# Where the operands of the matmuls lie in on-chip memory: start addresses by role, modulo 512 bytes

## The chip, the cores and the metric

The kernel runs on one core of a Trainium2 chip. The metric is the device time of one execution in microseconds (us); lower is better. The time before is 1484.54 us, the median of 3 runs.

## The reference: what is computed

Two encoder layers over 512 tokens of width 1024. Each layer adds a normed token mixer and a normed SwiGLU channel mixer; layer 0 mixes by neighbourhood attention, layer 1 by dilated attention in three groups.

```python
def reference(x, ...):
    for layer in range(DEPTH):
        j = layer // N_MIXERS
        h = rms_norm(x, norm_mix_pre[layer])
        if layer % N_MIXERS == 0:
            h = neighbourhood_attention(h, na_w_qkv[j], na_w_o[j], na_rpb[j])
        else:
            h = dilated_attention(h, dil_w_qkv[j], dil_w_o[j])
        x = x + rms_norm(h, norm_mix_post[layer])
        h = rms_norm(x, norm_ffn_pre[layer])
        x = x + rms_norm(swiglu(h, ffn_w_gate[layer], ffn_w_up[layer], ffn_w_down[layer]), norm_ffn_post[layer])
    return x
```

All of it is fp32. The sizes that count are the projections: D_MODEL 1024, D_FF 2816 (22 tiles of 128).

## The kernel before

**The products.** Every large product is done in three matmuls. `split` (L364) makes of an fp32 value a high part in the float32r format (ScalarE, L365) and the rest, also float32r (VectorE, L366). `mm3` (L376) then multiplies high by high (L377), high by low (L378) and low by high (L379):

```python
def mm3(o, s, m, start, stop):
    i = pe.matmul(o, s[0], m[0], start=start, stop=False, skip_group_check=True)
    pe.matmul(o, s[0], m[1], start=False, stop=False, skip_group_check=True)
    pe.matmul(o, s[1], m[0], start=False, stop=stop, skip_group_check=True)
```

The first operand, `s`, is the stationary one: its 128 columns are loaded as weights before each matmul (engine row PEld). The second, `m`, is the moving one: 256 or 512 columns stream through. While one matmul streams its moving operand, the weights of the next are read. On top of that, 2x2 blocks of a product are formed with seven products where eight would be usual (class `Seven`, L405, and `Values`, L479); four of the seven are `d1`, `s2`, `s4`, `s3` with operand sums.

**The stages**, in order, for each layer: the mixer (value products, then per head pair the query and key products `pp`, scores, softmax, transposes, values), the out-projection (`out_proj`, tiles `yo`), gate and up (`gate_up`, tiles `gu`, 22 units of 7 products of 12 matmuls of 256 columns: 1,848 matmuls) and down (`down`, tiles `yd_s` and `yd_pp`, 462 matmuls of 512 columns). The out-projection has 192 matmuls of 512 columns.

**The order of the work** on each engine is found by a planner (class `Order`, L131): it simulates the program with costs from `_cost` (L77) several times and pins the best order it found (L1441). It reads which columns of which buffer an instruction touches; it knows nothing of addresses.

**The places.** Buffers lie side by side on each partition in the order in which the pools are opened: first `ident` and `mhalf` (L306 to L308), then `rxa` (transposed activations of the moving side, L323), `rxc` (the same, and other things by stage, L324), `vmem` (L325), `mem` (L327), small values, then `wpool`: two raw weight buffers and eight slots for split weights (`wslot`, L369; tiles named `h_..` and `l_..`). The rest is an arena that grows from the left (`rxb`, `raw`) and from the right (`akl`, `ao`, `wm`, `memc`). The constant `mhalf` (128x1) takes 32 bytes, so that every buffer behind it starts 32 bytes past a multiple of 64. A piece of a buffer that a matmul reads starts at a multiple of 512 bytes from the buffer's start, with few exceptions (the queries of layer 0's odd heads: 256 more). So a matmul operand's start modulo 512, its residue below, is that of its buffer.

**Roles.** In `Seven`, stationary operands are weights (`wslot`, or `vmem` and the end of `rxc` for the product `s4`, by `w22_ring`, L347) and moving ones are activations (`rxa`, `rxc`, `rxb`). In `Values` and `v_quarter` it is the other way round. In `out_proj` the activations `rv` (in `rxa`) are stationary, the weights moving. In `down` the stationary operands are the activations split into `hl_` (L1047, in `rxc`), the moving ones are weights in `wslot`.

Of the kernel before, what the change touches and what calls it, by code (L numbers as in the profile page):

```python
# [13 lines left out]
F32 = mybir.dt.float32  # L14
F32R = mybir.dt.float32r
# [3 lines left out]
P = 128  # L19
SEQ = 512  # L20
D = 1024
# [7 lines left out]
COLS = 64  # L29
ROWS = 8  # L30
EPS = 1e-6
MEM, ARENA = 14544, 9 * D
NEG = -1e30
BIG = 3.0e38
X1A, X1B, X2B, D1, S2, S4, S3 = range(7)
BANKS = {"pp": 3, "s": 2, "t": 2, "o": 1}
SLOPES = [float(np.float32(2.0) ** np.float32(-8.0 * (h + 1) / HEADS)) for h in range(HEADS)]

# [258 lines left out]
def encoder_kernel(ctx: ExitStack, tc: tile.TileContext, a: dict, out: bass.AP):  # L297
    nc = tc.nc
    act, dve, pool, pe = nc.scalar, nc.vector, nc.gpsimd, nc.tensor

    cpool = ctx.enter_context(tc.tile_pool(name="cpool", bufs=1))
    wpool = ctx.enter_context(tc.tile_pool(name="wpool", bufs=4))
    psum = ctx.enter_context(tc.tile_pool(name="psum", bufs=1, space=bass.MemoryType.PSUM))
    dpool = ctx.enter_context(tc.tile_pool(name="dpool", bufs=1, space=bass.MemoryType.DRAM))

    ident = cpool.tile([P, P], F32, name="ident")  # L306
    make_identity(nc, ident)
    mhalf = cpool.tile([P, 1], F32, name="mhalf")  # L308
    dve.memset(mhalf, -0.5)
    spill = [dpool.tile([NT, P, D], F32, name=f"spill{i}") for i in range(3)]  # L310

    tags, arenas, extra = {}, [], []
# [1 line left out]
    def tagged(pool_, shape, dtype, tag, name, bufs):  # L314
        v = pool_.tile(shape, dtype, tag=tag, name=name, bufs=bufs)
        tags.setdefault(tag, ([], bufs))[0].append(v.tensor.name if hasattr(v, "tensor") else v.name)
        return v
# [4 lines left out]

    rxa = cpool.tile([P, 10 * D], F32R, name="rxa")  # L323
    rxc = cpool.tile([P, 5 * D + 256], F32R, name="rxc")  # L324
    vmem = cpool.tile([P, D], F32R, name="vmem")  # L325

    mem = cpool.tile([P, MEM], F32, name="mem")  # L327
    rvd = [dpool.tile([PAIRS, P, D], F32, name=f"rvd{i}") for i in range(2)]

    tops = {"left": 0, "right": 0}  # L330
# [1 line left out]
    @contextmanager  # L332
    def arena(name, n, side="left", dtype=F32):
        with tc.tile_pool(name=f"p_{name}", bufs=1, side=side) as pool_:
            v = pool_.tile([P, n], dtype, name=name)
            at = tops[side]
            tops[side] += n
            mine = [v.tensor.name if hasattr(v, "tensor") else v.name, at, at + n, len(arenas), None, side]
            arenas.append(mine)
            yield v  # L340
            mine[4] = len(arenas)
            tops[side] -= n

    def ring(mem, start, n, bufs):
        return cycle([mem[:, start + i * n:start + (i + 1) * n] for i in range(bufs)])

    def w22_ring(mem):  # L347
        return cycle([hl(vmem, 0, 512), hl(mem, 0, 512)])

    small_ = cycle(range(20))  # L350

    def small(name, n=1):
        if "o0" in name or "o1" in name:
            return tagged(cpool, [P, n], F32, f"small_o{next(small_)}", name, 1)
        return tagged(cpool, [P, n], F32, f"small{n}", name, 16 if n > 1 else 12)

    def load2(srcs, name, raw=None):
# [461 lines left out]
    def gate_up(layer, xs, hid, more, rings, sums):  # L819
        wg, wu = a["wg"], a["wu"]  # L820
        raws = ring(more, 0, 2 * D, 3)
        g_, u_, p5_ = rings
        v_ = w22_ring(rxc[:, 4 * D:5 * D])
        units, us = {}, {}

        def unit_of(f):
            if f in units or f >= FT:
                return units.get(f)
            raw = load2((wg[layer, f], wu[layer, f]), f"gu{layer}_{f}", None if f % 5 < 2 else next(raws))
            b, g = bank(("s", "s", "pp", "o", "pp", "pp")[f % 6], f"gu{layer}_{f}"), next(g_)  # L830

            def sink(n, left, other):
                u = us.get(f)
                if n == 0:
                    act.activation(g[:, :256], other, AF.Copy)
                    dve.tensor_add(g[:, :256], g[:, :256], left)
                elif n == 1:
                    act.activation(u[:, :256], other, AF.Copy)
                    dve.tensor_sub(u[:, :256], u[:, :256], left)  # L839
                elif n == 2:  # L840
                    dve.tensor_sub(u[:, 256:], other, left)
                else:
                    act.activation(g[:, :256], g[:, :256], AF.Silu)
                    act.activation(g[:, 256:], left, AF.Silu)
                    dve.tensor_mul(hid[f], *(v.rearrange("p (h c) -> p h c", h=2) for v in (g, u)))

            units[f] = Seven(raw, b, xs, f"{layer}_{f}", sink, None, next(v_), (pool, pool, dve, dve))
            return units[f]

        ahead, early = 3, 5  # L850
        for f in range(early):
            unit_of(f).first()
        for f in range(FT):
            for i in range(f, min(f + 2, FT)):
                if i not in us:
                    us[i], units[i].p5 = next(u_), next(p5_)
            run(unit_of(f), unit_of(f + 1), unit_of(f + ahead) if f + ahead >= early else None)
            if sums and (f < 16 or f % 2 == 0):
                sums.pop(0)(units[f].added)
# [151 lines left out]
    def hl(mem, i, n):  # L1011
        return mem[:, i * D:i * D + n], mem[:, i * D + n:i * D + 2 * n]
# [6 lines left out]
    xs = {i: op4(rxa, 2 * n) for n, i in enumerate((D1, S2, S4, S3, X2B))} | {X1A: op4(rxc, 0), X1B: op4(rxc, 2)}  # L1019
# [17 lines left out]
    def mix_out(layer, w, rxb, wm, load_x):  # L1037
        for j in range(PAIRS - 1):
            nc.gpsimd.dma_start(rxa[:, j * D:(j + 1) * D], rvd[layer][j])

        us = [None] * 2 + [hl(wm, 0, D), (wm[:, 2 * D:], vmem), hl(rxa, 8, D)] + [hl(rxb, 2 * i, D) for i in range(3)]

        out_proj(w, rv, layer, load_x, us, (ring(mem, 4 * D, D, 4), ring(mem, 0, D, 4), ring(mem, 13440, 512, 2)),
                 (mem[:, 11392:11392 + D], mem[:, 12416:12416 + D]))

    def ffn(layer, stack, memc):
        hl_ = ring(rxc, 0, D, 5)  # L1047
        rxb = None
        hm = mem[:, :FT * 512]
        h2 = hm.rearrange("p (h x) -> p h x", h=2)  # L1050
        hid = [h2[:, :, f * 256:f * 256 + 256] for f in range(FT)]
        with arena(f"raw{layer}", 6 * D) as more:
            gate_up(layer, xs, hid, more, (ring(memc, 0, 512, 5), cycle([memc[:, 2560:3072], mem[:, 13520:14032]]), ring(mem, MEM - 512, 256, 2)),
                    sums[layer])
            rcomb = ring(memc, 2 * D, 512, 2)

            def sink(t, xt, hs, gn):
                if layer == 1:
                    for n in range(2 if t == NT - 1 else 1):
                        s = slice(512 * n, 512 * n + 512) if t == NT - 1 else ALL  # L1060
                        (nc.sync, act)[n].dma_start(out[t][:, s], xt[:, s])
                else:
                    nc.sync.dma_start(spill[1][t], xt)
                    prenorm(hs[t], xt, gn, f"n{layer}_{t}")
                    operands(mixer_operands(rxb) if rxb is not None else None, x, hs, t, rcomb, f"n{layer}_{t}")

            end = down(layer, hm, hl_, memc[:, :2 * D], more, sink)
        if layer == 0:
            rxb = stack.enter_context(arena("rxb1", 6 * D, dtype=F32R))
        end()  # L1070
        return rxb
# [5 lines left out]
    rxb = stack.enter_context(arena("rxb0", 6 * D, dtype=F32R))  # L1077
# [23 lines left out]
    ost_, w22_ = ring(ao, 0, D, 1), w22_ring(ao[:, D:2 * D])  # L1101
# [3 lines left out]
    q_, k_, kl_ = ring(rxc, 0, 1152, 2), ring(rxc, 2304, D, 2), cycle([zero_rows(v) for v in (akl, rxc[:, 4352:])])  # L1105
    vq = [v_quarter(apv[:, qd * D:(qd + 1) * D], a["na_v"][qd], f"n{qd}",
                    raw0 if qd == 0 else None) for qd in range(4)]
    qs, ks, us = {}, {}, {}
# [36 lines left out]
             lambda v: v.rearrange("p (i c) -> p i c", i=ROWS))  # L1145

    inner.close()
    with arena("wm0", 3 * D, "right", F32R) as wm:
        mix_out(0, a["na_o"], rxb, wm, lambda xt, t: nc.sync.dma_start(xt, a["x_rows"][t]))
    stack.close()  # L1150
    memc = inner.enter_context(arena("memc0", 3 * D, "right"))
# [9 lines left out]
    pt_, few_ = ring(ap, 10 * D, D, 4), ring(mem, 0, 96, 2)  # L1161
    bt, qs, ks = memc[:, 0:1536].rearrange("p (k c) -> p k c", c=P), memc[:, 1536:2048], memc[:, 2048:2560]
    p5_ = ring(memc, 2560, 256, 2)
    q_, k_, kl_, ost_ = rxc[:, 0:D], rxc[:, D:2 * D], rxc[:, 2 * D:3 * D], ring(rxc, 3 * D, D, 1)
    w22_ = w22_ring(rxc[:, 4 * D:5 * D])
    def by_token(v):

        return v.rearrange("p (m r) -> p r m", r=4)
# [188 lines left out]
    order = [3 * j + g for j in range(PAIRS) for g in orders[j]]  # L1357
    stats, parts, weight, pts, vg, ready, left, later = {}, {}, {}, {}, {}, [], {}, {}

    vus, vslots = {}, cycle([hl(rxc, 0, D), hl(rxc, 2, D), (vmem, rxc[:, 4 * D:5 * D])])  # L1360
    for qd in range(2):
        v = v_quarter(ap[:, (6 + qd) * D:(7 + qd) * D], a["dil_v"][0, qd], f"d{qd}")
        nc.sync.dma_start(vd[0][qd].rearrange("t p c -> p t c"), v)
# [63 lines left out]
                nc.sync.dma_start(xt[32 * r + 16:32 * r + 32], rows[r, 0:16])  # L1427

    inner.close()
    with arena("wm1", 3 * D, "right", F32R) as wm:  # L1430
        mix_out(1, a["dil_o"], rxb, wm, load_block)
    stack.close()
    memc = inner.enter_context(arena("memc1", 3 * D, "right"))
# [90 lines left out]
```

## Time and profile before

| | before |
|---|---|
| median of 3 runs | 1484.54 us (1484.52 to 1489.98) |
| the profiled execution's own time | 1487.69 us |
| span in the profile | 1485.9 us |
| granted TensorE clock | 0.996 |
| PE busy | 1442.8 us (97%), 10788 instructions |
| DVE busy | 1196.8 us (81%) |
| ACT busy | 904.1 us (61%) |
| POOL busy | 542.4 us (37%) |

PE is TensorE's matmuls, PEld its weight loads, DVE VectorE, ACT ScalarE, POOL GpSimd. Matmuls overlap each other in the records (each has a modelled end), so what a matmul costs is not its duration but the time from its start to the next one's start; this distance is called the pace here. A row of the timeline has the start in us, the duration in us, engine, line, operation, and what is written from what: `gu<-rxa,h_b` writes bank `gu` from buffers `rxa` and `h_b`; two buffers of the same name are shown once. The windows table has for each stretch its length, then for each engine its busy time and in brackets its instructions, those that reach in over an edge counted too.

### The profile page before, as it was taken

The page shows a single profiled execution, that of the slowest core. Times are in us where ns is not written, and L with a number is a line of the kernel's source. Part 1 is how long each engine was busy: PE and PEld are TensorE (multiplying, and loading weights), DVE is VectorE, ACT ScalarE, POOL GpSimd, SP SyncE. Part 2 cuts the span into 40 slices and gives each one's busy share as a digit, 9 for nine tenths or more (in the row PEclk, how much of TensorE's full clock was granted, in tenths as well). Part 3 has the DMA queues.
Part 4 walks back from the last instruction along what each step waited for, and adds up shares of the span by engine and source line. Part 5 has one row for each costly group of instructions (what it writes and reads, how often), then busy time and mean ns, then how long its engine had stood idle before and what let it go on. Part 6 is the DMA issues. An engine that isn't in the chain of part 4 may idle for free.

```text
span 1485.9 us, 27934 instructions
## 1 busy us (share of the span) xinstructions
PE 1442.8 (97%) x10788; PEld 1333.1 (90%) x10788; DVE 1196.8 (81%) x1876; ACT 904.1 (61%) x1819; POOL 542.4 (37%) x398
## 2 busy tenths in 40 slices
PE   7999999899999999999999999999999999999997
PEld 6988877899999888899999999989977999999886
DVE  5499967699889788797689788787657989998877
ACT  4478874555555567544467778876675654555664
POOL 5345425544231001665555444334204644330001
PEclk9999999899999999999999999999999999999999
DMA  5346487677333664435433343333766788834662
GB/s 200 139 177 179 155 286 206 227 221 212 114 112 114 204 220 162 168 126 187 142 100 101 93 145 116 100 133 103 237 206 214 200 243 243 252 126 149 203 208 92
DMA packets 86645, 253.22 MB, mean 170 GB/s; under 512 B 19312, under 2 KB 31600, under 8 KB 84464
## 3 DMA queue, kind: packets, MB, share of 16 engines
q1 hardware_dynamic: 77696, 197.69, 40.4%
q0 software_dynamic: 8672, 53.48, 13.9%
q8 instruction: 85, 1.39, 0.4%
q14 instruction: 48, 0.39, 0.1%
q10 hardware_dynamic: 144, 0.26, 0.0%
HBM read 229.24 MB, written 68.29 MB: 200 GB/s over the span
## 4 chain that ended last, share of the span: by engine, by line
PE 77%; DVE 8%; ACT 7%; DMA 3%; issue 3%; POOL 1%; SPq 0%; POOLq 0%; DVEq 0%; ACTq 0%
PE gu L377 10%; PE gu L378 9%; PE gu L379 9%; PE pp_d L377 5%; PE pp_d L379 4%; PE pp_d L378 4%; PE yd_s L377 3%; PE yd_s L379 3%; PE yd_s L378 3%; PE yd_pp L377 2%; PE yd_pp L379 2%; PE yd_pp L378 2%; PE sb L1274 2%; PE yo L377 2%; PE yo L379 1%
## 5 line engine op out<-in xcount | busy, mean ns | idle before, releaser
L585 POOL TENSOR_TENSOR rs_yd<-v_yd,mhalf 128x1 f32<-128x1 f32 x8 | 8.3, 1043 | 261.3 <-DVE v_yd L583 261.3
L378 PE MATMUL gu<-rxa,h_b 128*128 128x256 f32 x352 | 100.0, 284 | 2.5 <-DVE rxa L602 2.5
L377 PE MATMUL gu<-rxc,h_a 128*128 128x256 f32 x352 | 99.7, 285 | 2.0 <-ACT h_a L365 1.2
L377 PE MATMUL gu<-rxa,h_c 128*128 128x256 f32 x352 | 99.7, 283 | 1.3 <-DVE memc L839 1.1
L378 PE MATMUL gu<-rxc,h_a 128*128 128x256 f32 x352 | 99.7, 284 | 1.2 <-DVE rxc L602 1.0
L377 PE MATMUL gu<-rxa,h_b 128*128 128x256 f32 x352 | 99.7, 284 | 1.2 <-ACT rxa L601 1.2
L379 PE MATMUL gu<-rxa,l_b 128*128 128x256 f32 x352 | 99.6, 283 | 0.2 <-DVE l_b L366 0.2
L379 PE MATMUL gu<-rxc,l_a 128*128 128x256 f32 x352 | 99.1, 282 | 0.0
L378 PE MATMUL gu<-rxa,h_c 128*128 128x256 f32 x352 | 98.7, 280 | 0.0
L379 PE MATMUL gu<-rxa,l_c 128*128 128x256 f32 x352 | 98.3, 280 | 0.0
L365 ACT ACTIVATE rxc<-mem 128x512 fp32r<-128x512 f32 (+2 forms) x90 | 55.9, 624 | 65.9 <-PE yd_pp L378 33.8
L445 POOL TENSOR_TENSOR r_d<-r_d 128x512 f32<-128x512 f32 x24 | 36.1, 1506 | 161.0 <-DVE l_ad L366 122.9
L445 POOL TENSOR_TENSOR r_gu<-r_gu 128x512 f32<-128x512 f32 x20 | 30.6, 1529 | 149.8 <-DVE l_a L366 102.4
L366 DVE TENSOR_TENSOR rxc<-mem,rxc 128x512 fp32r<-128x512 f32 (+2 forms) x90 | 64.4, 719 | 19.5 <-ACT rxc L365 19.2
L445 POOL TENSOR_TENSOR raw<-raw 128x512 f32<-128x512 f32 x24 | 38.0, 1582 | 99.4 <-DVE l_a L366 74.7
L378 PEld LDWEIGHTS gu<-rxa,h_b 128*128 128x128 f32 x352 | 67.6, 192 | 2.7 <-DVE rxa L602 2.7
L377 PEld LDWEIGHTS gu<-rxc,h_a 128*128 128x128 f32 x352 | 67.1, 192 | 2.8 <-ACT h_a L365 1.4
L377 PEld LDWEIGHTS gu<-rxa,h_c 128*128 128x128 f32 x352 | 66.5, 189 | 2.9 <-DVE memc L839 1.3
L378 PEld LDWEIGHTS gu<-rxc,h_a 128*128 128x128 f32 x352 | 67.2, 191 | 1.8 <-DVE rxc L602 1.8
L377 PEld LDWEIGHTS gu<-rxa,h_b 128*128 128x128 f32 x352 | 67.3, 192 | 1.5 <-ACT rxa L601 1.4
L1238 ACT ACTIVATE mem<-mem 128x256 f32<-128x256 f32 x128 | 63.8, 504 | 7.5 <-DVE mem L1237 7.3
L379 PEld LDWEIGHTS gu<-rxa,l_b 128*128 128x128 f32 x352 | 67.4, 191 | 0.4 <-DVE l_b L366 0.4
(610 smaller groups left out, 6157.7 us busy)
## 6 DMA issues: line engine op xcount, KB each, us to landing
wsum<-wd POOLq DMA_DIRECT2D x24, 1408.0 KB, 12.1
r_d<-dil_qk SPq DMA_DIRECT2D x48, 512.0 KB, 4.1
raw<-wg SPq DMA_DIRECT2D x24, 512.0 KB, 5.1
raw<-wu SPq DMA_DIRECT2D x24, 512.0 KB, 8.4
wsum<-wsum POOLq DMA_DIRECT2D x8, 1408.0 KB, 10.3
raw<-wsum SPq DMA_DIRECT2D x22, 512.0 KB, 4.3
r_gu<-wg SPq DMA_DIRECT2D x20, 512.0 KB, 3.8
r_gu<-wu SPq DMA_DIRECT2D x20, 512.0 KB, 4.9
```

What stands on the lines that cost most here:

```text
L365: act.activation(h, src, AF.Copy)
L366: dve.tensor_sub(l, src, h.bitcast(F32))
L377: i = pe.matmul(o, s[0], m[0], start=start, stop=False, skip_group_check=True)
L378: pe.matmul(o, s[0], m[1], start=False, stop=False, skip_group_check=True)
L379: pe.matmul(o, s[1], m[0], start=False, stop=stop, skip_group_check=True)
L445: self.added = e[0].tensor_add(q[0], q[0], q[2])
L585: pool.tensor_tensor(r, v, mhalf, op=ALU.pow)
L1238: act.activation(pr[:, f], pr[:, f], AF.Exp, bias=st[:, c:c + 1], scale=-1.0, accum_out=st[:, c + 2:c + 3])
L1274: pe.matmul(ss[hd][:, f0:f0 + P], qf[rw, block(c)], kf[rw, block(c)], start=True, stop=True)
```

## The change

The change moves buffers. No instruction is added or taken away.

- `mhalf` leaves the head of the memory for a pool of its own behind `wpool` (and takes 256 bytes); what stood behind it starts 32 bytes earlier, at multiples of 64.
- `mem` and `vmem` change places, and `mem` is 16 columns shorter; the 20 single-column values of the out-projections become columns of one tile, `few_small`.
- `rxc` is used through a view `rxs` that starts 64 columns (256 bytes) later, for the `s4` weights, for the keys and value operands, and for `hl_` in `down`. The activations in `rxc` in `gate_up`, and the queries of layer 1, stay at its start.
- `wm` is 88 columns longer, so that it starts 352 bytes earlier.

```diff
-MEM, ARENA = 14544, 9 * D
+MEM, ARENA = 14528, 9 * D + 88
+SHIFT = 64
...
+    zpool = ctx.enter_context(tc.tile_pool(name="zpool", bufs=1))
...
-    mhalf = cpool.tile([P, 1], F32, name="mhalf")
-    dve.memset(mhalf, -0.5)
...
+    mem = cpool.tile([P, MEM], F32, name="mem")
     vmem = cpool.tile([P, D], F32R, name="vmem")
-    mem = cpool.tile([P, MEM], F32, name="mem")
+    few_small = cpool.tile([P, 32], F32, name="few_small")
+    mhalf = zpool.tile([P, 64], F32, name="mhalf")[:, 0:1]
+    dve.memset(mhalf, -0.5)
+    rxs = rxc[:, SHIFT:SHIFT + 5 * D]
...
-    small_ = cycle(range(20))
+    small_ = cycle([few_small[:, i:i + 1] for i in range(20)])
...
-            return tagged(cpool, [P, n], F32, f"small_o{next(small_)}", name, 1)
+            return next(small_)
...
-        v_ = w22_ring(rxc[:, 4 * D:5 * D])
+        v_ = w22_ring(rxs[:, 4 * D:])
...
-        hl_ = ring(rxc, 0, D, 5)
+        hl_ = ring(rxs, 0, D, 5)
...
-    with arena("wm0", 3 * D, "right", F32R) as wm:
+    with arena("wm0", 3 * D + 88, "right", F32R) as wm:
...
-    q_, k_, kl_, ost_ = rxc[:, 0:D], rxc[:, D:2 * D], rxc[:, 2 * D:3 * D], ring(rxc, 3 * D, D, 1)
-    w22_ = w22_ring(rxc[:, 4 * D:5 * D])
+    q_, k_, kl_, ost_ = rxc[:, 0:D], rxs[:, D:2 * D], rxs[:, 2 * D:3 * D], ring(rxs, 3 * D, D, 1)
+    w22_ = w22_ring(rxs[:, 4 * D:])
...
-    vus, vslots = {}, cycle([hl(rxc, 0, D), hl(rxc, 2, D), (vmem, rxc[:, 4 * D:5 * D])])
+    vus, vslots = {}, cycle([hl(rxs, 0, D), hl(rxs, 2, D), (vmem, rxs[:, 4 * D:])])
```

The residues (start address modulo 512 bytes) in the two built programs:

| buffer | before | after |
|---|---|---|
| `ident` (transposes) | 128 | 128 |
| `rxa`; `rxc` at its start | 160 | 128 |
| `rxs` (`rxc` 256 bytes on) | - | 384 |
| `vmem` | 160 | 384 |
| `mem` | 160 | 128 |
| slots for split weights (`h_`, `l_`) | 480 | 384 |
| `rxb`, `raw` (left arena) | 480 | 128 |
| `wm` | 480 | 128 |
| `akl`, `ao`, `memc` (right arena) | 480 | 480 |

All residues before except that of `ident` are 32 more than a multiple of 64; after, those of the first eight rows are multiples of 64.

For split matmuls that follow each other with equal width, the distance from the residue of the weights being loaded (for the next matmul) to that of the operand that streams meanwhile, counted over the built programs:

| width | distance | pairs before | pairs after |
|---|---|---|---|
| 256 columns | 0 | 1624 | 14 |
| 256 columns | 192 | 4816 | 0 |
| 256 columns | 320 | 1202 | 0 |
| 256 columns | 256 | 0 | 7583 |
| 256 columns | 160 | 0 | 45 |
| 512 columns | 0 | 70 | 1183 |
| 512 columns | 320 | 1204 | 0 |
| 512 columns | 256 | 0 | 91 |

The order of the instructions stays as it was on all engines, apart from the end of layer 0's `gate_up`, where the planner sees that other columns of `mem` are shared. There TensorE's rows in the program before are these (`gu0_20` and `gu0_21` are the banks of the last two units; `h_b`, `l_b`, `h_c`, `l_c` split weights):

```order
L379 MATMUL gu0_21_5096<-rxa_76,l_b0_21_5341 128x256
L377 MATMUL gu0_21_5096<-rxa_76,h_b0_21_5340 128x256
L378 MATMUL gu0_21_5096<-rxa_76,h_b0_21_5340 128x256
L379 MATMUL gu0_21_5096<-rxa_76,l_b0_21_5341 128x256
L377 MATMUL gu0_20_4980<-rxa_76,h_c0_20_5318 128x256
L378 MATMUL gu0_20_4980<-rxa_76,h_c0_20_5318 128x256
```

and in the changed program, from the same place on:

```order
L385 MATMUL gu0_21_5072<-rxa_77,l_b0_21_5317 128x256
L383 MATMUL gu0_21_5072<-rxa_77,h_b0_21_5316 128x256
L383 MATMUL gu0_20_4956<-rxa_77,h_c0_20_5294 128x256
L384 MATMUL gu0_20_4956<-rxa_77,h_c0_20_5294 128x256
L385 MATMUL gu0_20_4956<-rxa_77,l_c0_20_5295 128x256
L383 MATMUL gu0_20_4956<-rxa_77,h_c0_20_5294 128x256
```

Twelve matmuls of unit 20 move two places ahead, before the last two of unit 21's group; after that a few evictions and splits of ScalarE and VectorE swap places with their neighbours. The lines of the changed kernel are 6 higher here (L383 for L377).

More of the change, by code (lines that the diff above doesn't have):

```diff
@@ L1039, in mix_out @@
             nc.gpsimd.dma_start(rxa[:, j * D:(j + 1) * D], rvd[layer][j])
-        us = [None] * 2 + [hl(wm, 0, D), (wm[:, 2 * D:], vmem), hl(rxa, 8, D)] + [hl(rxb, 2 * i, D) for i in range(3)]
+        us = [None] * 2 + [hl(wm, 0, D), (wm[:, 2 * D:3 * D], vmem), hl(rxa, 8, D)] + [hl(rxb, 2 * i, D) for i in range(3)]
         out_proj(w, rv, layer, load_x, us, (ring(mem, 4 * D, D, 4), ring(mem, 0, D, 4), ring(mem, 13440, 512, 2)),
@@ L1052, in ffn @@
         with arena(f"raw{layer}", 6 * D) as more:
-            gate_up(layer, xs, hid, more, (ring(memc, 0, 512, 5), cycle([memc[:, 2560:3072], mem[:, 13520:14032]]), ring(mem, MEM - 512, 256, 2)),
+            gate_up(layer, xs, hid, more, (ring(memc, 0, 512, 5), cycle([memc[:, 2560:3072], mem[:, 13504:14016]]), ring(mem, MEM - 512, 256, 2)),
                     sums[layer])
@@ L1429, in encoder_kernel @@
     inner.close()
-    with arena("wm1", 3 * D, "right", F32R) as wm:
+    with arena("wm1", 3 * D + 88, "right", F32R) as wm:
         mix_out(1, a["dil_o"], rxb, wm, load_block)
```

## The prediction

> **What bounds the kernel now.** I read the page first: the span, the busy times, and the chain that ended last.
>
> ```profile
> span 1485.9 us, 27934 instructions
> PE 1442.8 (97%) x10788; PEld 1333.1 (90%) x10788; DVE 1196.8 (81%) x1876; ACT 904.1 (61%) x1819; POOL 542.4 (37%) x398
> PE 77%; DVE 8%; ACT 7%; DMA 3%; issue 3%; POOL 1%; SPq 0%; POOLq 0%; DVEq 0%; ACTq 0%
> ```
>
> TensorE carries 77% of the chain. The windows table, cut at the stages, shows where another engine comes near it: the first gate-up (282 to 482 us), the first down, the value products of layer 1, its attention, and the second gate-up.
>
> ```profile
> 282.00:482.00 200.00, 198.86 (x1660) 198.16 (x1661) 177.37 (x228) 104.47 (x181) 64.10 (x43) 0.98 0.54 166
> 482.00:640.00 158.00, 154.90 (x874) 134.73 (x873) 131.11 (x163) 97.44 (x150) 36.44 (x22) 1.00 0.59 190
> 640.00:735.00 95.00, 92.87 (x791) 91.92 (x790) 75.85 (x55) 42.98 (x55) 56.48 (x24) 1.00 0.44 145
> 735.00:1100.00 365.00, 359.62 (x3027) 334.05 (x3027) 282.15 (x603) 267.73 (x682) 143.67 (x97) 1.00 0.42 128
> 1165.00:1365.00 200.00, 198.45 (x1672) 197.19 (x1671) 181.37 (x231) 104.86 (x184) 71.88 (x50) 1.00 0.74 211
> ```
>
> The columns after the length are PE, PEld, DVE, ACT, POOL. In the gate-ups PE idles about 1 us of 200, and DVE is busy 177 and 181 us: close behind. So the time is set by the pace of the matmuls, and the change can act only there: it adds, removes and reorders next to nothing. The same table for TensorE alone, over 150 us inside the first gate-up, gives that pace:
>
> ```profile
> 320.00:470.00 150.00, 150.00 (x1273) 1.00 0.49 150
> ```
>
> 150.00 / 1273 = 117.8 ns per matmul of 256 columns, with no idle time. The timeline says that this isn't one pace but several, each held for many matmuls. Four rows of the first gate-up; I counted the matmuls between them:
>
> ```profile
> 299.21 0.28 PE L379 MATMUL gu<-rxa,l_c 128*128 128x256 f32 x1
> ...
> 305.22 0.28 PE L377 MATMUL gu<-rxa,vmem 128*128 128x256 f32 x1
> ...
> 305.82 0.28 PE L379 MATMUL gu<-rxa,vmem 128*128 128x256 f32 x1
> ...
> 315.62 0.28 PE L377 MATMUL gu<-rxc,h_a 128*128 128x256 f32 x1
> ...
> 324.57 0.28 PE L377 MATMUL gu<-rxa,vmem 128*128 128x256 f32 x1
> ```
>
> From 299.21 to 305.22 are 53 matmuls: 6.01 / 53 = 113.4 ns. Their weights (`h_`, `l_`) have residue 480, their moving operand 160. Then come the weights in `vmem`, residue 160 like the moving `rxa`: 5 matmuls in 0.60 us, 120 ns each. From 315.62 on the residues are 480 and 160 again, but the pace doesn't come back: 76 matmuls in 8.95 us, 117.8 ns. Equal residues elsewhere, here both 480:
>
> ```profile
> 712.03 0.28 PE L378 MATMUL vd<-l_cd,rxb 128*128 128x256 f32 x1
> ...
> 714.79 0.28 PE L377 MATMUL vd<-rxc,rxa 128*128 128x256 f32 x1
> ```
>
> 23 matmuls in 2.76 us are 120.0 ns. So equal residues cost 6.6 ns against 113.4, and a stream that passed through such a group goes on at 117.8, as if the two readers had fallen into a worse step. In the one place shown the quick pace ended with the first `vmem` group.
>
> **The change part by part.**
>
> *Distances at 256 columns.* Of the pairs in the front's table, 1624 had equal residues, and 14 are left. That takes away the groups that run at 120 and, by the reading above, what throws the stream from 113.4 to 117.8. New is the distance of 256, in nearly all pairs. In the trace it stands only in short runs, such as the scores of an odd head, whose queries start 256 bytes later (weights 416, moving operand `rxc` 160):
>
> ```profile
> 91.01 0.28 PE L718 MATMUL s<-rxc 128*128 128x256 f32 x1
> 91.12 0.28 PE L719 MATMUL s<-akl,rxc 128*128 128x256 f32 x1
> 91.24 0.29 PE L377 MATMUL pp_n<-rxa,h_an 128*128 128x256 f32 x1
> ```
>
> 0.11 and 0.12 us: within what the other distances show, too short to hold a step. The nearest long row is the one of the same instruction at 113.4 ns, and I take that. The other ends are 120.0 above, and below it the transposes, whose moving operand `ident` is the only one that starts at a multiple of 64 in this trace. Their row merges 8, and the line's own median duration is in the second row:
>
> ```profile
> 855.65 1.04 PE L1334 MATMUL t<-ident,mem 128*128 128x128 f32 x8
> ...
> L1334 PE MATMUL t<-ident,mem x256: 270/272/332, 807.8 to 1114.9; 128*128 128x128 f32 x128
> ```
>
> (1040 - 272) / 7 = 110 ns, also with 128 columns of weights each. It is another kind of matmul, so it is an end and not the value. How many matmuls are there? Each of the three lines of `mm3` has 3036 records, and 1308 of the sum are 512 columns wide:
>
> ```profile
> 0.00:1486.00 1486.00, 894.87 (x3036) 570.20 (x3036) 1.00 0.55 170
> 0.00:1486.00 1486.00, 96.27 (x384) 1.00 0.55 170
> 0.00:1486.00 1486.00, 124.59 (x528) 1.00 0.55 170
> 0.00:1486.00 1486.00, 94.74 (x396) 1.00 0.55 170
> ```
>
> (The first row is L377, the others `yo`, `yd_s` and `yd_pp`.) 3 x 3036 - 1308 = 7800 of 256 columns. Their mean pace is 117.8 in the gate-up and 92.87 / 791 = 117.4 among the value products; I take 117.5. From 117.5 to 113.4 are 4.1 ns x 7800 = 32.0 us. What TensorE saves counts where it ends the chain: x 0.77 = 24.6 us. The rest is waited away behind DVE, ACT and DMA, which are next in the chain.
>
> *Distances at 512 columns.* Down and half of the out-projection go the other way, from 320 to equal residues. Three places:
>
> ```profile
> 500.27 0.39 PE L377 MATMUL yd_pp<-h_d0p,rxc 128*128 128x512 f32 x1
> ...
> 505.76 0.39 PE L377 MATMUL yd_pp<-h_d0p,rxc 128*128 128x512 f32 x1
> ...
> 1392.18 0.40 PE L377 MATMUL yd_s<-h_d1p,rxc 128*128 128x512 f32 x1
> ...
> 1399.88 0.40 PE L377 MATMUL yd_s<-h_d1p,rxc 128*128 128x512 f32 x1
> ```
>
> 24 matmuls in 5.49 us are 229 ns, 33 in 7.70 us are 233 ns, both at a distance of 320. With equal residues (`yo<-rxa`, both operands in one buffer):
>
> ```profile
> 237.87 0.39 PE L377 MATMUL yo<-rxa 128*128 128x512 f32 x1
> ...
> 239.23 0.40 PE L377 MATMUL yo<-rxb,rxa 128*128 128x512 f32 x1
> ```
>
> 6 in 1.36 us, 227 ns. So equal residues don't hurt here. Between 227 and 233, from a mean of 231, 1308 matmuls lose 2.6 us at most and gain 5.2; I take 0.
>
> *The starts at multiples of 64.* No split matmul of this trace has such a start, so its effect alone is bounded by the transposes' 110 below and by 0 (no matmul reads more bytes than before, so a loss has no cause in it). I take 0; the other end is a rival.
>
> *The rest.* `few_small` and the longer `mhalf` change none of the 28 operations on single columns; a wait that is added there would stand on POOL, which is busy 37%. The twelve matmuls that move ahead in the first gate-up issue the same work, in a stage in which PE idles 1.1 us of 200 in all; at most that much comes or goes. ACT, DVE and the DMAs read and write the same pieces at new starts. No row shows what they would do there; from the windows DVE, the fullest of them, has 19 to 83 us of room per stage, so a few per cent either way is covered by the matmuls. I take 0 for all of it.
>
> The sum: 24.6 us off the profiled execution's 1487.69 gives 1463.1. That execution is 3.15 us over the median of the runs, so the median after is forecast at 1484.54 - 24.6 = 1459.9, rounded to **1460 us**.
>
> **The rivals.**
>
> *Much faster: aligned starts bring the pace to that of the transposes.* If a start 32 bytes past a multiple of 64 costs each stream an extra access, all split matmuls gain. At 110 ns: 7.5 x 7800 = 58.5 us; at 220 for 512 columns: 11 x 1308 = 14.4 us; together 72.9 x 0.77 = 56 us. But a gate-up then needs 200 - 1660 x 0.0075 = 187.5 us of TensorE, against 177 and 181 us of DVE, whose work is a chain of splits behind ScalarE: I take a further 9 us off. 47 us less: 1437 us. For it: 113.4 is still above 110, and every split matmul has the odd 32. Against it: the transposes' rows are the only sign. In the Trainium skill, TensorE: Matmul & The Clock Gate, section Back-to-back issue gap, an isolated warm matmul is given as N / 2.4 + 2.5 ns, so 109 ns for 256 columns and 216 for 512. By that page the estimate would be 8.5 x 7800 + 15 x 1308 = 86 us of TensorE, before what the other engines take.
>
> *No change: the place has no say, or the slow step remains.* If the paces come from something else, such as who starts when after a stop, then 117.5 stays and the time is 1484.5; if all go to 117.8, 0.3 x 7800 x 0.77 = 1.8 us more. For it: the same residues (480, 160) run at 113.4 and at 117.8 in one stage. Against it: 120.0 stands exactly where the residues are equal. The Trainium skill is on this rival's side: SBUF — State Buffer, section Who interferes with whom, gives TensorE two independent read ports, one for the moving operand and one for the weights, and says "PE and ACT never wait on anyone". By that rule no place could matter; the 120.0 against 113.4 above disagrees with it.
>
> *Slower: a distance of 256 is a bad one.* The moving operand passes 1024 bytes while the weights' 512 are read, so from a distance of 256 the two readers meet in the middle of every matmul instead of near an end. If meeting costs what equal residues cost, all 256-column matmuls run at 120.0: 2.5 x 7800 x 0.77 = 15 us, 1499.5 us. It decides once the pace is above 117.5. For it: distance 256 is untried in a long stream. Against it: the scores' 0.11 and 0.12 us, and that 192 and 320, on both sides of it, both hold 113.4 at times.
>
> **How the numbers follow.** 0.5% is 7.4 us, about what a measurement of this kernel can tell from no change. The forecast (1460) has 0.40: it rests on rows of the same instruction. Much faster (1437) has 0.32, no change (1484.5) 0.17, slower (1499.5) 0.11. Faster by over 0.5% are the first two, 0.72; within 0.5% 0.17; slower 0.11. The range runs from 1428, the much faster case without what I take off for DVE (1484.5 - 56), to 1487, the no-change case with its 1.8 us. It leaves out the slower case and the tail below.
>
> **What would show it.** Right: in the changed profile the windows table inside a gate-up gives about 113.4 ns per matmul (some 1323 in 150 us) before and after the `vmem` groups alike, and no run at 120; DVE idles less; the downs hold 227 to 233. The much faster case shows 110 or less and PE waiting for DVE's splits in the gate-ups. Wrong: 117.8 or 120 in long streams, or downs above 233.

## The result, and the profile after

The changed kernel takes **1498.82 us** (median of 5 runs, 1496.4 to 1502.2) against 1489.98 for the kernel before on the same chip (median of 5, 1484.52 to 1493.61): a ratio of 1.0069, 95% interval 1.0048 to 1.009. So the change made it slower by about 0.7%. The forecast was 1460; the rival "slower: a distance of 256 is a bad one" had 1499.5.

The page after, same lines as before:

```profile
span 1495.7 us, 27934 instructions
PE 1455.0 (97%) x10788; PEld 1351.0 (90%) x10788; DVE 1195.4 (80%) x1876; ACT 904.5 (60%) x1819; POOL 540.6 (36%) x398
PE 76%; DVE 10%; ACT 8%; DMA 4%; issue 2%; SPq 0%; POOLq 0%; POOL 0%; DVEq 0%; ACTq 0%
```

The span grew by 9.8 us and TensorE's busy time by 12.2, with the same 10788 matmuls. DVE and ACT moved by 1.4 us and less. So the matmuls themselves became slower. The windows table of the kernel after, cut at the same times, says where:

```profile
282.00:482.00 200.00, 199.44 (x1646) 199.12 (x1647) 176.27 (x227) 104.14 (x180) 63.95 (x44) 0.99 0.53 165
482.00:640.00 158.00, 155.31 (x869) 136.15 (x869) 130.02 (x163) 97.54 (x150) 33.81 (x21) 0.99 0.59 187
640.00:735.00 95.00, 94.27 (x785) 93.86 (x783) 73.79 (x53) 42.01 (x54) 55.18 (x23) 1.00 0.45 148
735.00:1100.00 365.00, 359.16 (x3004) 335.37 (x3004) 279.91 (x600) 266.78 (x681) 145.16 (x98) 1.00 0.40 123
1165.00:1365.00 200.00, 197.99 (x1641) 196.86 (x1640) 179.19 (x227) 103.79 (x182) 78.09 (x54) 1.00 0.71 206
```

In the second gate-up TensorE is busy as long as before (198 us of 200) and gets through 1641 matmuls where it did 1672; in the first it is busier than before and does 1646 where it did 1660. The granted clock is 0.99 to 1.00 in these windows (0.98 to 1.00 before), so it isn't the clock. The paces stand in the timeline of the kernel after (L383 to L385 are the three lines of `mm3`):

```profile
312.83 0.28 PE L385 MATMUL gu<-rxa,l_c 128*128 128x256 f32 x1
...
455.03 0.28 PE L385 MATMUL gu<-rxc,l_a 128*128 128x256 f32 x1
...
505.03 0.39 PE L384 MATMUL yd_pp<-l_d0p,rxc 128*128 128x512 f32 x1
...
513.19 0.39 PE L384 MATMUL yd_s<-l_d0p,rxc 128*128 128x512 f32 x1
...
661.95 0.28 PE L384 MATMUL vd<-rxc,rxb 128*128 128x256 f32 x1
...
700.95 0.28 PE L385 MATMUL vd<-h_dd,rxa 128*128 128x256 f32 x1
...
729.36 0.28 PE L383 MATMUL pp_d<-rxa,h_ad 128*128 128x256 f32 x1
...
1081.16 0.28 PE L385 MATMUL pp_d<-rxa,l_cd 128*128 128x256 f32 x1
...
1150.91 0.38 PE L383 MATMUL gu<-rxc,h_a 128*128 128x256 f32 x1 [0.74 <-ACT rxc L607]
...
1386.13 0.28 PE L385 MATMUL gu<-rxa,l_c 128*128 128x256 f32 x1
...
1404.00 0.39 PE L384 MATMUL yd_s<-l_d1p,rxc 128*128 128x512 f32 x1
...
1412.16 0.39 PE L384 MATMUL yd_s<-l_d1p,rxc 128*128 128x512 f32 x1
```

From 312.83 to 455.03 the trace has 1185 matmuls: 142.20 / 1185 = 120.0 ns each, without one that differs. The value products from 661.95 to 700.95 are 325 in 39.00 us, 120.0 again. The pace that equal residues had in short groups before now holds in nearly all long runs of 256 columns. The 512-column matmuls went the other way: 36 in 8.16 us at both places in the downs are 227 ns, where 229 and 233 stood. For the other rows, the same two stages in the kernel before:

```profile
726.05 0.28 PE L377 MATMUL pp_d<-rxa,h_ad 128*128 128x256 f32 x1
...
1072.65 0.28 PE L379 MATMUL pp_d<-rxa,l_cd 128*128 128x256 f32 x1
...
1142.70 0.38 PE L377 MATMUL gu<-rxc,h_a 128*128 128x256 f32 x1 [0.74 <-ACT rxc L601]
...
1373.39 0.28 PE L379 MATMUL gu<-rxa,l_c 128*128 128x256 f32 x1
```

The query, key and attention stage of layer 1 went from 346.6 to 351.8 us, the second gate-up from 230.7 to 235.2: 9.7 us in the two. For the whole account I took the time from each matmul's start to the next one's over both traces and counted as pace what is up to 126 ns at 256 columns and up to 240 at 512. About 7700 gaps at 256 columns went from a mean of 117.15 to 119.76 ns, 20 us more; about 1250 at 512 from 230.9 to 227.2, 5 us less; the longer gaps (stalls), set right for their count, gave back about 6. The sum is +9, against a span of +9.8.

### The profile page after: what moved, and what is told of

It is laid out like the page before. It is cut to its first block, busy times and chain, and to the rows that moved or that the text cites. A ratio compares the mean times of both kernels' runs of the same rounds, so it can differ in the third digit from the quotient of the medians.

```text
span 1495.7 us, 27934 instructions
## 1 busy us (share of the span) xinstructions
PE 1455.0 (97%) x10788; PEld 1351.0 (90%) x10788; DVE 1195.4 (80%) x1876; ACT 904.5 (60%) x1819; POOL 540.6 (36%) x398
## 4 chain that ended last, share of the span: by engine, by line
PE 76%; DVE 10%; ACT 8%; DMA 4%; issue 2%; SPq 0%; POOLq 0%; POOL 0%; DVEq 0%; ACTq 0%
PE gu L383 9%; PE gu L384 9%; PE gu L385 9%; PE pp_d L383 4%; PE pp_d L385 4%; PE pp_d L384 4%; PE yd_s L384 3%; PE yd_s L385 3%; PE yd_s L383 3%; PE yd_pp L384 2%; PE yd_pp L385 2%; PE yd_pp L383 2%; PE vd L383 2%; PE vd L384 2%; PE vd L385 2%
## 5 line engine op out<-in xcount | busy, mean ns | idle before, releaser
L591 POOL TENSOR_TENSOR rs_yd<-v_yd,mhalf 128x1 f32<-128x1 f32 x8 | 9.5, 1185 | 258.9 <-DVE v_yd L589 258.9
L383 PE MATMUL gu<-rxa,h_b 128*128 128x256 f32 x352 | 100.2, 286 | 1.2 <-ACT rxa L607 1.2
L383 PE MATMUL gu<-rxc,h_a 128*128 128x256 f32 x352 | 99.9, 285 | 1.4 <-ACT rxc L607 0.7
L383 PE MATMUL gu<-rxa,h_c 128*128 128x256 f32 x352 | 100.1, 285 | 0.5 <-DVE memc L845 0.4
L385 PE MATMUL gu<-rxa,l_b 128*128 128x256 f32 x352 | 100.1, 285 | 0.2 <-DVE l_b L372 0.2
L385 PE MATMUL gu<-rxc,l_a 128*128 128x256 f32 x352 | 99.4, 283 | 0.0
L385 PE MATMUL gu<-rxa,l_c 128*128 128x256 f32 x352 | 99.3, 283 | 0.0
L383 PEld LDWEIGHTS gu<-rxc,h_a 128*128 128x128 f32 x352 | 67.3, 192 | 2.3 <-ACT rxc L607 1.3
L383 PEld LDWEIGHTS gu<-rxa,h_b 128*128 128x128 f32 x352 | 67.9, 193 | 1.5 <-ACT rxa L607 1.4
L383 PEld LDWEIGHTS gu<-rxa,h_c 128*128 128x128 f32 x352 | 67.4, 192 | 1.7 <-DVE memc L845 0.6
L385 PEld LDWEIGHTS gu<-rxa,l_b 128*128 128x128 f32 x352 | 68.1, 193 | 0.4 <-DVE l_b L372 0.4
```

What stands on the lines that cost most here:

```text
L591: pool.tensor_tensor(r, v, mhalf, op=ALU.pow)
```

## The experiments

Theory A: the distance between the two operands sets the pace, and 256 counts as 0. Theory B: the distance doesn't matter; what is bad is that both operands start at multiples of 64. A third reading, the reason that the slower rival gave: at 256 the two readers meet in the middle of a matmul.

**Streams alone.** The kernel leaves out the whole computation of the reference. It issues streams of 48 matmuls of 256 columns (36 of 512) in the order of `mm3`, one stream for each distance, with the moving operand at a multiple of 64 (`even_`) or 32 past it (`odd_`). The letter is the distance / 32, so `g` is 192 and `i` is 256. Its core:

```python
m0 = 8 * odd
w0 = 9 * D + (m0 - 8 * step) % 128
...
for s, m in ((0, 0), (0, 1), (1, 0)):
    mv = m0 + m * 4 * D + k * 512
    st = w0 + s * D + k * P
    pe.matmul(o, big[:, st:st + P], big[:, mv:mv + width], ...)
```

> Computes nothing of the reference: only streams of split-format matmuls with the other engines at rest, 48 of 256 columns (36 of 512) for each distance from the weights' residue to the moving operand's, in steps of 32 bytes, once with the moving operand at a multiple of 64 (even) and once 32 past one (odd). Theory A, the distance decides, and 256 counts as 0: even and odd alike hold 120 ns per matmul at 0 and at 256, and 113 to 118 elsewhere. Theory B, starts at multiples of 64 are what is bad: even streams hold 120 at all distances, odd ones 120 at 0 only. At 512 columns both expect 227 to 233, Theory A with the low value at 0 and 256.

Timeline of this run, of each stream the later part (the first 20 or so matmuls settle in), merged to one row: start, length from the first start to the last end, count.

```profile
225.50 3.52 PE L44 MATMUL even_a<-big 128*128 128x256 f32 x28
264.46 3.22 PE L44 MATMUL even_g<-big 128*128 128x256 f32 x27
277.17 3.52 PE L44 MATMUL even_i<-big 128*128 128x256 f32 x28
367.81 3.22 PE L44 MATMUL odd_g<-big 128*128 128x256 f32 x27
380.52 3.52 PE L44 MATMUL odd_i<-big 128*128 128x256 f32 x28
432.83 5.38 PE L44 MATMUL wide_a<-big 128*128 128x512 f32 x23
460.75 5.52 PE L44 MATMUL wide_g<-big 128*128 128x512 f32 x23
469.66 5.83 PE L44 MATMUL wide_i<-big 128*128 128x512 f32 x25
```

The last matmul of a row takes 0.28 us (0.39 at 512 columns), so distance 0 is (3.52 - 0.28) / 27 = 120.0 ns, 192 is (3.22 - 0.28) / 26 = 113.1 (113.3 by the starts themselves), and 256 is (3.52 - 0.28) / 27 = 120.0 again, even and odd alike. Over the second half of each stream, from the starts:

| distance modulo 256 | 0 | 32 | 64 | 96 | 128 | 160 | 192 | 224 |
|---|---|---|---|---|---|---|---|---|
| 256 columns, ns | 120.0 | 116.7 | 117.8 | 120.0 | 118.5 | 118.6 | 113.3 | 118.3 |
| 512 columns, ns | 226.7 | - | 228.9 | - | 232.0 | - | 233.3 | - |

Each value stands for a distance and for 256 more, at both alignments, and none of these differs from its twins by more than 0.1 ns (the very first stream left out, which began the program at 213 ns). Of the four places at 512 columns 0 is the best and 192 the worst, the other way round from 256 columns; 64 is better than 128 at both widths. Theory B falls here, and with it the "much faster" rival: neither alignment gave 110.

**The changed kernel with other distances.** A gap ahead of `vmem` moves everything behind it, and `SHIFT` moves the parts in `rxc` along; the tile of `mhalf` shrinks by as much, so that the arena stays. For a distance of 192 the gap is 16 columns:

```diff
-SHIFT = 64
+SHIFT = 80
...
+    gap = cpool.tile([P, 16], F32, name="gap")
+    dve.memset(gap, 0.0)
     vmem = cpool.tile([P, D], F32R, name="vmem")
...
-    mhalf = zpool.tile([P, 64], F32, name="mhalf")[:, 0:1]
+    mhalf = zpool.tile([P, 48], F32, name="mhalf")[:, 0:1]
```

For 128 it is 32 columns, for 64 48, for 32 56 (`SHIFT` 96, 112, 120). For 0 it is 64 columns, `SHIFT` is 128, and `mhalf` lies in the gap. The pairs of the main kind (6193, weights from the slots, `vmem` or `rxs`) are then at that distance. The reversed kind (1390, the value products of layer 1 above all, where weights and activations change roles) is at the negative of it: 320 for 192, which is 64 modulo 256. The 512-column pairs have nearly all equal residues throughout.

> The changed kernel with a gap of 64 bytes, so that starts stay at multiples of 64 and the distances become 192 and 320 in place of 256. Theory A (distance): long streams at 113.4 to 117.8 ns in place of 120.0; 7600 matmuls x 2.3 to 6.6 x 0.77 = 13 to 39 us less than the changed kernel, 1460 to 1485 us. Theory B (starts): 120.0 stays, 1499 us.

The timeline of the kernel at 192:

```profile
313.48 0.34 PE L385 MATMUL gu<-rxa,rxc 128*128 128x256 f32 x1
313.66 0.28 PE L386 MATMUL gu<-rxa,rxc 128*128 128x256 f32 x1
313.78 0.28 PE L387 MATMUL gu<-rxa,rxc 128*128 128x256 f32 x1
...
427.90 0.28 PE L387 MATMUL gu<-rxa,l_b 128*128 128x256 f32 x1
...
1268.55 0.35 PE L385 MATMUL gu<-rxa,h_c 128*128 128x256 f32 x1
1268.74 0.28 PE L386 MATMUL gu<-rxa,h_c 128*128 128x256 f32 x1
1268.85 0.28 PE L387 MATMUL gu<-rxa,l_c 128*128 128x256 f32 x1
...
1322.57 0.28 PE L386 MATMUL gu<-rxa,h_b 128*128 128x256 f32 x1
```

969 matmuls in 114.12 us from 313.78 on, 117.8 ns, in the first gate-up, and 474 in 53.72 from 1268.85 on, 113.3 ns, in the second: same instruction, same distance, two steps. Directly ahead of each of the two runs stands a gap between two starts, of 180 and 190 ns; the 108 matmuls before the first gap ran at 113.3. Not every such gap changes the step: of 24 gaps of 126 to 400 ns in this trace that have a dozen matmuls at one of the two paces on either side, 9 did and 15 did not. The time is 1480.13 us (median of 10, 1476.48 to 1484.2), ratio 0.994 (0.9922 to 0.9957): faster than both kernels.

> The same with a gap of 128 bytes: distances 128 and 384, starts at multiples of 64. Theory A with a period of 256: 113.4 to 117.8 ns as at 192, 1460 to 1485 us; if the period is 128, 120.0 and 1499 us. Theory B (starts): 120.0, 1499 us.

At 128 it is 1493.82 us (1489.51 to 1496.02), ratio 1.0028 (1.0014 to 1.0042). The windows table for TensorE, 110 us inside the first gate-up; the count takes in each matmul that overlaps the window, one or two too many:

```profile
315.00:425.00 110.00, 110.00 (x929) 1.00 0.57 173
```

110.00 / 929 = 118.4, the 118.5 of the streams. But this isn't its only pace. In the second gate-up:

```profile
1190.00:1245.00 55.00, 55.00 (x461) 1.00 0.80 239
```

55.00 / 460 = 119.6 by the window, and by the starts 503 matmuls from 1184.95 to 1245.30 at 120.0, behind a gap of 199 ns. So 120.0 is not the mark of equal residues alone: 128 has two steps, 118.5 and 120.0, and the streams showed only the first. The time came out as neither branch of the expectation had it (1460 to 1485, or 1499).

> The changed kernel with all operands 32 bytes later: distance 256 stays, starts are 32 past a multiple of 64 as before the change. Theory A (distance): 120.0 ns stays, 1499 us. Theory B (starts): 113.4 to 117.8 ns, 1460 to 1485 us.

Nearly all operands 32 bytes further (a tile of 8 columns at the head, `ARENA` and `wm` 8 columns shorter), distance 256 kept: 1499.48 us (1494.34 to 1499.87), ratio 1.0067 (1.0043 to 1.0091). Its row for the same window:

```profile
315.00:425.00 110.00, 110.00 (x919) 1.00 0.58 178
```

119.7 by the window, as after the change at multiples of 64. So Theory B doesn't hold in the kernel either.

> The changed kernel with 256 bytes more between the two kinds, so that nearly all pairs of 256 columns (7597) have equal residues instead of a distance of 256. If the distance counts modulo 256, this is the same kernel to the chip: 120.0 ns in the streams, 227 ns at 512 columns, and the time of the changed kernel, 1498.8 us within 0.3%. If 256 is bad for a reason of its own (the two readers meeting in the middle of each matmul, the reason that the prediction gave for its slower rival), then equal residues, which meet at the ends, give another pace and a time at least 0.5% from 1498.8.

With equal residues it is 1497.33 us (1495.12 to 1500.4), ratio 1.0054 (1.0034 to 1.0073), 0.1% from the changed kernel, and its long run in the first gate-up is:

```profile
313.20:455.20 142.00, 142.00 (x1186) 1.00 0.52 159
```

142.00 / 1185 = 119.8 by the window; the starts give 120.0. So 256 is no bad place of its own: it is the same place as 0. The meeting in the middle, the reason that the rival gave, isn't needed; and at 512 columns 0 and 256 are equal again and are the best of the places in the table, which it doesn't describe.

**Does a group of equal residues throw the stream behind it?** Streams alone again, none of the reference's work: 48 matmuls at a distance, 12 at distance 0 without a stop, 48 at the first distance (`fine_` streams; `ex` is 64, `mx` is 192).

```python
for step in range(32):
    stream(256, ((2 * step, 4), (0, 1), (2 * step, 4)), f"fine_{LETTERS[step // 2]}{'xy'[step % 2]}")
```

> Streams of matmuls alone; nothing of the reference is computed. First: 48 matmuls of 256 columns at a distance (every multiple of 8 bytes from 0 to 248), then without a stop 12 at distance 0, then 48 at the first distance again. Where the pace is set by the distance alone, the third part runs at the pace of the first: at 192 113.3 ns before and after the 12, at 64 117.8, at 128 118.5. Where a group of equal residues also throws the stream that follows into a worse step, as the prediction read the first gate-up, 192 runs at 113.3 before and at 117.8 after. Distances between the multiples of 32 lie between their neighbours (between 113.3 and 118.8 from 160 to 192) if the pace follows the place smoothly; if it goes by steps of 32 or 64 bytes, they repeat a neighbour's value. At 512 columns: 226.7 to 233.3 at every multiple of 16, the same at a distance and 256 past it.

Timeline rows of the later part of the first and of the third part, for 64 and for 192:

```profile
126.33 3.81 PE L44 MATMUL fine_ex<-big 128*128 128x256 f32 x31
...
133.23 3.79 PE L44 MATMUL fine_ex<-big 128*128 128x256 f32 x32
...
343.24 4.02 PE L44 MATMUL fine_mx<-big 128*128 128x256 f32 x34
...
350.30 4.05 PE L44 MATMUL fine_mx<-big 128*128 128x256 f32 x33
```

At 192: (4.02 - 0.28) / 33 = 113.3 ns before the group and (4.05 - 0.28) / 32 = 117.8 after it. So the prediction's reading of the first gate-up is shown. But at 64 it is the other way: (3.81 - 0.28) / 30 = 117.7 before and (3.79 - 0.28) / 31 = 113.2 after. Both places have the same two steps; from rest the stream at 192 takes the quick one and at 64 the slow one, and a disturbance changes it. Further streams had other groups of 12 inside. A group at 32, 64 or 128 inside a stream at 192 didn't throw it (113.3 before and after); in a stream at 64 a group at 192 brought it from 117.8 to 113.3, and one at 32 or 128 left it at 117.8. With the group at 0, the third part ran as the first, within 0.1 ns, at 32, 96 and 128; it didn't at 160 (118.6, then 117.3), nor at several multiples of 8, such as 88 (120.0, then 113.3), 168 (113.3, then 116.7) and 232 (118.6, then 121.9). By multiples of 8 the paces don't lie smoothly between their neighbours: 116.7 at 48 and 56, 120.0 at 40, 113.3 at 168 and 118.8 at 176 in the first parts. At 512 columns, by multiples of 16, they went from 226.6 (at 0 and at 112) to 234.5 (at 160), a little past the 233.3 that was expected; so the order of the four places in the table is no rule for those between them.

> The changed kernel with 192 bytes more between the two kinds: distance 64 in 6193 pairs and 448 in 1390 (192 modulo 256). If the distance modulo 256 sets the pace, the long streams run at 117.8 ns or, once thrown, at 113.3, as the streams alone showed for 64 and 192, and nowhere at 120: mean between 116 and 117.5, which with 5 us per ns (1498.8 to 1480.1 us for 119.7 to 116.0 ns) gives 1480 to 1488 us. If 192 is a good place of its own, and the steps are its own, 64 runs at 117.8 throughout: 1489 us.

1485.46 us (1481.32 to 1487.19), ratio 0.998 (0.9967 to 0.9993). Windows table at a long run of each step:

```profile
310.00:424.00 114.00, 114.00 (x970) 1.00 0.60 182
950.50:960.40 9.90, 9.90 (x90) 1.00 0.42 108
```

114.00 / 968 = 117.8, and by the starts 89 matmuls from 950.40 at 113.4. The time is in the range. The slow step, the one from rest, holds most of this kernel: its 256-column gaps up to 126 ns have a mean of 117.2 ns, against 115.9 in the kernel at 192, and that is why it is behind 192.

> The changed kernel with 224 bytes more between the two kinds: distance 32 in 6193 pairs and 480 in 1390 (224 modulo 256). By the streams alone: 116.7 ns in the main streams, before and after a disturbance alike, and 118.3 in the value products of layer 1, a mean of about 117.0 and by 5 us per ns 1485 us (1481 to 1489). No run at 113.3 and none at 120. If instead what counts is only that the residues differ by a multiple of 64, the time is that of one of the others: 1480 or 1494 us, with runs at 113.3 or 118.5.

1486.25 us (1481.64 to 1488.59), ratio 0.9985 (0.9971 to 0.9999). Here too two runs:

```profile
437.50:453.00 15.50, 15.50 (x134) 1.00 0.20 69
1259.00:1342.00 83.00, 83.00 (x714) 1.00 0.65 193
```

83.00 / 712 = 116.6, the 116.7 that was expected, but 15.50 / 132 = 117.4 (by the starts 137 matmuls at 117.8) was not: 32 has a second step as well, which the streams alone didn't show. It isn't rare: from 1185.06 us on 397 matmuls in a row have a mean of 117.8. The time came as expected, since 117.8 is only 1.1 ns from 116.7: the mean over the kernel is 117.3, where 117.0 was expected.

All kernels together, each against the kernel before on its own chip:

| distance of the main kind | paces in long runs, ns | mean of gaps up to 126 ns | us | ratio |
|---|---|---|---|---|
| 0 | 120.0 | 119.8 | 1497.33 | 1.0054 |
| 256 (the change) | 120.0 | 119.8 | 1498.82 | 1.0069 |
| 256, starts 32 further | 120.0 | 119.7 | 1499.48 | 1.0067 |
| 128 | 118.5, 120.0 | 118.8 | 1493.82 | 1.0028 |
| 192, 64 and 0 (before) | 117.8, 113.4, 120.0 | 117.2 | - | 1 |
| 32 | 116.7, 117.8 | 117.3 | 1486.25 | 0.9985 |
| 64 | 117.8, 113.4 | 117.2 | 1485.46 | 0.998 |
| 192 | 113.3, 117.8 | 115.9 | 1480.13 | 0.994 |

The kernel before has the mean of those at 32 and 64 and is a little slower than they are; its 512-column matmuls are also slower, 230.9 ns against 227.7 to 227.9.

## Why the prediction was wrong

**What bounds the kernel** was right: the pace of the matmuls set the time, and the change acted there.

**Distances at 256 columns** is the step that failed. It priced the new distance of 256, which no long stream of the trace showed, by "the nearest long row", that "of the same instruction at 113.4 ns". That row belongs to another place, 192. By the streams, distance 256 is the place of the row at 120.0, the equal residues that the change was to remove. Where the sum had 7800 x -4.1 ns x 0.77 = -24.6 us, the matmuls measured +2.6 ns on about 7700, 20 us more of TensorE time. Two of its readings hold: 120.0 is what equal residues cost, and a group of them throws a stream at 192 into 117.8. But the conclusion that the quick pace would stay once such groups are gone doesn't: in the kernel at 192, without them, 969 matmuls in a row still ran at 117.8. There the step changed at some of the short gaps, as at the two ahead of its long runs.

**Distances at 512 columns** was taken as 0, between 5.2 us of gain and 2.6 of loss; it was a gain at nearly that end (230.9 to 227.2 ns, about 5 us). **The starts at multiples of 64** as 0: right. **The rest** as 0: TensorE's stalls got shorter by about 6 us in all, as one expects where it is the slower side (argued, no run isolates it). With that and the 5 us at 512 columns, 20 us of pace became 9.8 of span, less than the 0.77 that was taken from the chain.

**The rivals.** "Slower" had the place and the price: all 256-column matmuls at 120.0, and 1499.5 us where 1498.82 was measured. Its working had 15 us over the median before, where the medians differ by 8.8 and the spans by 9.8. With two more runs the median before is 1489.98, 5 us above that of the three from which the prediction started, so that this rival's closeness in the time is partly luck. Its reason isn't shown: equal residues, which don't meet in the middle, cost the same as 256. What it counted against itself, the 0.11 and 0.12 us of the scores, was indeed too short to speak. "No change" falls with its two legs: the place does have a say, and the pace that came was 120.0 and not 117.8. The Trainium skill's rule in SBUF — State Buffer, section Who interferes with whom, that TensorE has two independent read ports, disagrees, as the prediction read it, with the streams alone: nothing else ran there on TensorE's operands, and the place of the weights moved the pace from 113.3 to 120.0 ns. By the estimate of 109 ns for an isolated matmul, from the Trainium skill, TensorE: Matmul & The Clock Gate, section Back-to-back issue gap, the matmuls would beat every measured pace: 113.3 at 256 columns and 226.6 at 512 (there 216) are the best of all distances tried.

The range left out the slower case, although the text itself named 120.0 as an end for an untried distance. With 120.0 as an end that nothing excluded, the range should have reached 1499.5.

What stays open: why the period is 256 bytes, what the two steps are physically, and which stall brings which step. The steps are read from one traced execution of each kernel, so how they fall in the other executions is not shown either. No run shows more than the paces.

## What to carry to other kernels

A price for a place, size or distance that the trace doesn't show can't be borrowed from the row of another one because the instruction is the same; take both ends into the range, or measure the streams alone first, a run of 0.6 ms that here would have given 120.0 for 256. It wouldn't have given the second steps, which stood in no stream from rest at the same place. For this kind of float32r stream, with weights loaded beside each matmul, lay out weights and moving operand by their distance modulo 256: of the places tried in the whole kernel, 192 was the best for 256 columns (ratio 0.994, ahead of 64 and 32), and equal residues were good for 512 columns (227.2 against 230.9 ns). "Apart" is not by itself good: 256 apart was the same as not apart at all.

## What the runs showed of the hardware

- The pace of such a stream depends on the distance from the weights being loaded to the moving operand modulo 256 bytes. By multiples of 32, in streams from rest, it is 113.3 (at 192) to 120.0 ns (at 0 and 96) at 256 columns; by multiples of 64 it is 226.7 (at 0) to 233.3 (at 192) at 512.
- It has memory: at 64 and 192 the same stream runs at 113.3 or 117.8 ns, at 32 at 116.7 or 117.8, at 128 at 118.5 or 120.0, for hundreds of matmuls in most of these cases. A group at distance 0 switches it at 64 and at 192. In the kernel at 192 the step also changed at 9 of 24 gaps of 126 to 400 ns, which no run isolates.
- Starts at multiples of 64 or 32 past them made no difference (streams within 0.1 ns; kernels 1.0069 and 1.0067).
